# A two-layer encoder trunk on one core: the places of the tiles in SBUF

## The chip, the core and the metric

The kernel runs on one core of a Trainium2 chip. A core has five engines that run apart from each other and meet in semaphores: TensorE (PE in the profile; its loads of the stationary operand are listed apart, as PEld), VectorE (DVE), ScalarE (ACT), GpSimd (POOL) and SyncE (SP), which here issues all transfers. The operands lie in SBUF, 128 partitions with the same byte addresses in each; products land in eight PSUM banks. The metric is the time of one execution on the chip in microseconds, the median of several runs.

## The reference, cut to what matters

Two sequences of 256 tokens with 1024 features (512 tokens in all) go through two layers. All arithmetic is float32.

```python
for i in range(DEPTH):                       # 2
    h = rms_norm(x, norm_mix[i])
    kv = rms_norm(mem, norm_mem[i]) @ w_mem_kv[i]
    if i % 2 == 0:
        p = h @ a_w_in[j]                    # differential attention, 8 heads
        mixed = diff_mixer(p[..., :-X_WIDTH], ...); w_out = a_w_out[j]
    else:
        p = h @ b_w_in[j]                    # three dilated windows, 8 heads each
        mixed = dilated_mixer(p[..., :-X_WIDTH], ...); w_out = b_w_out[j]
    cross = memory_attention(xq, mk, mv)
    x = x + concatenate([mixed, cross]) @ w_out
    x = x + conv_ffn(rms_norm(x, norm_ffn[i]), w_up[i], conv_w[i], conv_b[i], w_down[i])
```

## The kernel before, in words

**Products.** A float32 number is kept as two parts, hi and lo, each in a format that TensorE takes in one pass. A product of two such numbers is three matmuls (`mm3`, L368 to L370): hi by hi, hi by lo, lo by hi. Nearly all matmuls are 128 rows by 128 columns of stationary operand with 512 columns of moving operand. In a row of the profile `acc<-wh,hl` the first name behind the arrow is the moving operand and the second the stationary one, which a weight load (PEld) brings into the array before.

**Tiles.** `hh` and `hl` (`const` pool, [128, 8, 512], 16 KB for each partition) hold hi and lo of the normalised, transposed activations. `X` is the residual. Everything else that TensorE reads in these products lies in numbered slots of the pool `pool`: 30 slots `blk` of 2 KB, six `wh` and six `wl` of 4 KB (hi and lo of a weight unit), three `raw` of 4 KB (the unit as it is loaded), and slots `qn`, `e`, `eT`, `on`, `sq`.

**The three kinds of product.** They differ in which tiles meet in the array:

- the projections (`proj`, `proj_first`): moving `wh`/`wl`, stationary `hh`/`hl` (rows `acc<-wh,hh`, `acc<-wl,hh`, `acc<-wh,hl`);
- the up products of the FFN (`up_products`): moving `hh`/`hl`, stationary `wh`/`wl` (rows `acc<-hh,wh`, `sc<-hl,wh` and so on);
- the down products of the FFN, the output projections and the products with the memory tokens: moving `wh`/`wl`, stationary `blk` (rows `acc<-wh,blk` and so on).

**Order.** Coroutines on estimated engine clocks (`Sched`) write out one fixed order for each engine when the program is built. Weight units (220 of 512 KB) are loaded ahead by SP, split by ACT (L345) and DVE (L347). Projections and attention are interleaved in both layers; the FFN stands by itself.

**Places.** A pool gives its tiles addresses one behind the other, rounded up to 32 bytes; `const` comes first, then `pool` (each slot at its first use), then `small`. Some 128 bytes of constants stand at 16384, so `const` begins at 16512.

Of the kernel before, what the change touches and what calls it, by code (L numbers as in the profile page):

```python
# [24 lines left out]
NFF = DFF // 128  # L25
# [12 lines left out]

# [1 line left out]
class Event:  # L40
# [53 lines left out]
class Slots:  # L94
    """Buffers of one kind, handed out in the order in which they come free."""

# [70 lines left out]

# [1 line left out]
def unit_plan():  # L169
    """[(name, layer, rows, cols)] of [128, 1024] units: row blocks x column ranges."""  # L170
    plan = []
# [26 lines left out]
    def granules(name, layer, halves):  # L198
        """halves of 256 columns, two at a time."""
        for i in range(0, len(halves), 2):  # L200
            cols = sum(halves[i:i + 2], [])
            if i + 1 < len(halves):
                for u in range(4):
                    plan.append((name, layer, range(2 * u, 2 * u + 2), cols))
            else:
                proj(name, layer, cols)
# [55 lines left out]
def trunk_kernel(ctx: ExitStack, tc: tile.TileContext, io: dict, out: bass.AP):  # L262
# [3 lines left out]
    const = ctx.enter_context(tc.tile_pool(name="const", bufs=1))  # L266
    pool = ctx.enter_context(tc.tile_pool(name="pool", bufs=1))
    small = ctx.enter_context(tc.tile_pool(name="small", bufs=6))
    psum = ctx.enter_context(tc.tile_pool(name="psum", bufs=1, space=bass.MemoryType.PSUM))
# [24 lines left out]

# [1 line left out]
    X = const.tile([128, NT, D], F32, name="X")  # L296
# [7 lines left out]

    ident = const.tile([128, 128], F32, name="ident")
    perm_fwd = const.tile([128, 128], F32, name="perm_fwd")
    perm_bwd = const.tile([128, 128], F32, name="perm_bwd")
    mask = const.tile([128, 2, 512], BF16, name="mask")
    mhalf = const.tile([128, 32], F32, name="mhalf")
    gcols = const.tile([128, 12], F32, name="gcols")  # L310
    subg = const.tile([128, 128], F32, name="subg")
    convT = const.tile([128, 2, 4, 2 * NFF], F32, name="convT")
    nc.vector.memset(mhalf, -0.5)
# [10 lines left out]

# [1 line left out]
    plan = unit_plan()  # L326
# [45 lines left out]

# [1 line left out]
    def row_scale(src, h):  # L374
        """1 / rms of the rows of src [two of [128, 512]]; h: two slots for the squares."""
        ss = sm(2, "ss")
        for j in range(2):
            nc.scalar.activation(h[j].v, src[j], AF.Square, scale=1.0 / 32, accum_out=ss[:, j:j + 1])  # L378
            t = S.op("ACT", c_act(512, 0, 1))
        yield t  # L380
        rstd = sm(1, "rstd")
        s1 = sm(1, "s1")
        nc.gpsimd.tensor_scalar(s1, ss[:, 0:1], ss[:, 1:2], EPS, ALU.add, ALU.add)  # L383
        nc.gpsimd.tensor_tensor(rstd, s1, mhalf[:, 0:1], ALU.pow)
        yield S.op("POOL", 0.6)
        return rstd

    def norm_transposed(src, gkey, ident_, evac, src_done=None):
        """src: two of [128, 512]; evac(j, bank) is a coroutine that empties a bank of 4 blocks."""
        g = gains[gkey]  # L390
# [45 lines left out]
    def norm_h(t, gkey, permuted, x_ev, h_ev):  # L436
        """normalises token tile t of X into columns of hh, hl."""
        yield x_ev
# [42 lines left out]

# [1 line left out]
    CH = 2  # L483

    def fan_out(t, bank, posts):
        """hands the halves of a bank to their parts; frees the bank behind the last."""
        left = [len(posts)]

        def done(te):
            left[0] -= 1  # L490
            if not left[0]:
                bank.done(te)

        for j, p in enumerate(posts):
            S.spawn(p(t, bank.v[:, 256 * j:256 * j + 256], done))

    def proj(name, posts, h_evs=None, permuted=False):
        """one or two halves of 256 columns; post(t, slice, done) is spawned for each token tile."""
        n = len(posts)
# [23 lines left out]
    def proj_first(name, posts, h_evs):  # L523
        """proj of two halves with units and token tiles in the order FIRST."""
        bks, ws, seen = {}, [], [0] * NT
# [20 lines left out]
    class QBlock:  # L546
        """two heads; a[h]: hi of head h on its own partitions, lo on the other head's."""

# [7 lines left out]
    class KBlock:  # L556
        """two heads; a[h]: hi of head h on all partitions; lo: both heads' lo on their partitions."""

# [10 lines left out]
    def block_evac(kind, bufs, tp, g):  # L569
        """empties a bank of two heads into its block."""  # L570
        if kind == "-":
# [24 lines left out]
    def qk_post(rope, gcol, kinds, ev):  # L596
        """rms norm per head, rope, transposes; ev gets the two feature-major blocks."""
        qns = [None] * 2
# [86 lines left out]

# [1 line left out]
    def mem_tiles(l, evs):  # L687
        """normalised, transposed memory tiles; evs[i] gets [(hi, lo)] of two banks."""
        t = yield from load_gain(("mem", l), io["norm_mem"][l])
# [55 lines left out]

# [1 line left out]
    def transpose_e(e, n):  # L747
        """e: slot whose first n blocks of 128 columns are transposed; returns the slot of the result."""
        eT = yield from eT_s.get()
# [12 lines left out]
    def seq_view(x, s, permuted):  # L762
        """columns of sequence s of a [128, 512] tile; (q, b, r) of the permuted order in natural places."""
        if permuted:
            return x.rearrange("p (s b q r) -> p s q b r", s=2, q=2, r=2)[:, s]
        return x[:, s * 256:s * 256 + 256]

    def evac_seq(src, hi, lo, s, permuted):
        """PSUM [128, 256] of sequence s to hi, lo."""
        if permuted:  # L770
# [7 lines left out]
    def out_T(o, cols, tiles, s, permuted):  # L778
        """blocks at cols[j][i] of the slot o (token tile i of sequence s) to feature-major tiles[j]."""
        tp = yield from tp_s.get()  # L780
# [25 lines left out]
    def softmax2(sc):  # L806
        """two softmax numerators of 256 keys; scores are negated."""
        v = sc.v.rearrange("p (m k) -> p m k", m=2)
# [15 lines left out]
    def scores(sc, parts):  # L824
        """parts: (column, q block, q columns, k block, k columns); the two heads side by side in the array."""
        for c, q, tq, k, ks in parts:
# [243 lines left out]

# [1 line left out]
    def add_x(ps, t, c, ev, last):  # L1072
# [34 lines left out]
    def out_proj_last(name, groups, x_evs):  # L1107
        """several row groups, sequence by sequence."""
        ws = []
# [27 lines left out]

# [1 line left out]
    def ffn_post(l, i, bks, ev):  # L1139
# [139 lines left out]

# [1 line left out]
    for t in range(NT):  # L1281
# [24 lines left out]
    S.spawn(start())  # L1306
    nlam = const.tile([128, 1], F32, name="nlam")
    ropes = {}

    def setup():  # L1310
# [9 lines left out]
        yield 18.0  # L1320
        # gains of q (scaled and negated) and k, feature-major; 1 on the rotated dims
        nc.vector.tensor_scalar(gcols[:, 0:6], gcols[:, 0:6], QS, None, ALU.mult)
# [6 lines left out]
        nc.vector.tensor_tensor(lampr, lampr, lv[:, :, 1, :], ALU.mult)  # L1329
        lams = sm(2, "lams")  # L1330
        nc.vector.tensor_reduce(lams, lampr, AX.X, ALU.add)
        yield S.op("DVE", 1.0)
        lame = sm(2, "lame")
        nc.scalar.activation(lame, lams, AF.Exp)
# [34 lines left out]
    for key in ("aq", "ak", "b0", "b1", "b2"):  # L1369
        ropet = const.tile([128, 2, 2, 2, 16], F32, name=f"rope_{key}")  # L1370
        ropes[key] = ropet
    def gc(*cols):
        return [gcols[:, c:c + 1] for c in cols]

    # columns of gcols: xq l0, xq l1, a_q, b_q0..2 | xk l0, xk l1, a_k, b_k0..2
    G_XQ, G_AQ, G_BQ = (0, 1), 2, (3, 4, 5)
    G_XK, G_AK, G_BK = (6, 7), 8, (9, 10, 11)

    def main():
        ev = S.event  # L1380
        # layer 0
        xq, mk, mv = ev(), ev(), ev()
# [29 lines left out]
        yield from ffn(0, h1, x2, mT, [qk_post(None, gc(G_XK[1], G_XK[1]), "kk", mk), v_post(mv)])  # L1412
        # layer 1
        cross = [ev(), ev()]
# [25 lines left out]
def constants():  # L1440
    """Arrays that depend on the shapes alone."""
    f = np.float32
    ident = np.eye(128, dtype=f)
    j = np.arange(128)
    # token j = a*16 + r16*4 + r4 of a tile goes to column r4*32 + r16*8 + a
    a, r16, r4 = j // 16, (j % 16) // 4, j % 4
    fwd = np.zeros((128, 128), f)
    fwd[j, r4 * 32 + r16 * 8 + a] = 1
    # permuted row j = r4*64 + r16*16 + a of a tile goes to column a*8 + r16*2 + r4
    r4, r16, a = j // 64, (j % 64) // 16, j % 16  # L1450
# [54 lines left out]
```

## Time and profile before

| | |
|---|---|
| median of 3 runs | 1450.37 us (1450.26 to 1450.9) |
| span of the profiled execution | 1447.8 us |
| median less that span | 2.6 us |
| PE busy | 1420.1 us, 98% |
| PEld, DVE, ACT, POOL busy | 81%, 58%, 44%, 23% |
| mean share of the DMA engines | 27.9% |

The profile gives one execution's span, from its first to its last instruction; what the measured time has beside it is the third row. A matmul is recorded from its start to its modelled end, 0.39 us for 512 columns, while the next one starts some 0.23 us later, so PE's busy share hides small gaps, and the pace is read from the starts.

### The profile page before, as it was taken

How to read it: one execution, taken by the hardware profiler on the slowest of the kernel's cores; microseconds unless marked ns; L12 is line 12 of the kernel's file. 1: busy time of each engine (PE TensorE's matmuls, PEld its weight loads, DVE VectorE, ACT ScalarE, POOL GpSimd, SP SyncE). 2: the span in 40 equal slices, each digit the busy share in tenths (PEclk: the TensorE clock that was granted, in tenths of full speed). 3: DMA queues.
4: the chain of work that ended last, by engine and by line, in shares of the span. 5: the costliest groups of instructions: out<-in, count | busy, mean ns of one | idle time of the engine just before them, and what ended most of it. 6: DMA issues, size and time to landing. Idle time of an engine off the chain costs nothing.

```text
span 1447.8 us, 19017 instructions
## 1 busy us (share of the span) xinstructions
PE 1420.1 (98%) x7168; PEld 1169.7 (81%) x7168; DVE 841.1 (58%) x1314; ACT 642.8 (44%) x1177; POOL 338.2 (23%) x652
## 2 busy tenths in 40 slices
PE   6999999999999999999999999999999999999999
PEld 4778888879888888878878878888888888888887
DVE  5777778886654355446666435444476563466353
ACT  5666555545442244244446434444554432243231
POOL 5836554121000000030154065445130000000000
PEclk9999999999999999999999999999999999999999
DMA  6531131123332332434221221112223233323221
GB/s 221 163 97 49 31 102 59 59 73 105 104 98 92 98 98 92 130 104 131 69 92 55 67 69 59 60 63 80 77 88 100 90 96 93 102 87 103 87 73 58
DMA packets 39260, 129.33 MB, mean 89 GB/s; under 512 B 4608, under 2 KB 5504, under 8 KB 39168
## 3 DMA queue, kind: packets, MB, share of 16 engines
q1 hardware_dynamic: 39168, 128.11, 27.9%
q8 instruction: 57, 0.93, 0.3%
q14 instruction: 35, 0.29, 0.1%
HBM read 126.00 MB, written 2.10 MB: 88 GB/s over the span
## 4 chain that ended last, share of the span: by engine, by line
PE 89%; POOL 4%; DVE 2%; issue 2%; DMA 1%; ACT 1%; SPq 0%; POOLq 0%; DVEq 0%; ACTq 0%
PE acc L368 18%; PE acc L370 17%; PE acc L369 17%; PE sc L370 7%; PE sc L368 7%; PE sc L369 7%; PE tp L752 2%; PE o L1035 2%; PE sc L832 1%; PE sc L830 1%; PE tp L651 1%; POOL rstd L617 1%; PE tp L412 1%; PE o L369 1%; PE o L368 1%
## 5 line engine op out<-in xcount | busy, mean ns | idle before, releaser
L347 DVE TENSOR_TENSOR wl<-raw,wh 128x1024 fp32r<-128x1024 f32 x220 | 273.0, 1244 | 247.5 <-ACT wh L345 246.8
L345 ACT CAST wh<-raw 128x1024 fp32r<-128x1024 f32 x220 | 230.8, 1050 | 367.2 <-PE sc L369 191.7
L368 PE MATMUL acc<-wh,hh 128*128 128x512 f32 (+1 forms) x536 | 218.3, 407 | 0.9 <-ACT hh L425 0.9
L369 PE MATMUL acc<-wl,hh 128*128 128x512 f32 (+1 forms) x536 | 204.8, 382 | 0.0
L370 PE MATMUL acc<-wh,hl 128*128 128x512 f32 (+1 forms) x536 | 204.7, 382 | 0.0
L368 PE MATMUL acc<-wh,blk 128*128 128x512 f32 x368 | 148.8, 404 | 0.0
L368 PE MATMUL acc<-hh,wh 128*128 128x512 f32 (+1 forms) x384 | 145.1, 378 | 0.0
L368 PE MATMUL sc<-hh,wh 128*128 128x512 f32 (+1 forms) x384 | 144.9, 377 | 0.0
L369 PE MATMUL sc<-hl,wh 128*128 128x512 f32 (+1 forms) x384 | 144.5, 376 | 0.0
L370 PE MATMUL acc<-hh,wl 128*128 128x512 f32 (+1 forms) x384 | 144.5, 376 | 0.0
L369 PE MATMUL acc<-hl,wh 128*128 128x512 f32 (+1 forms) x384 | 144.5, 376 | 0.0
L370 PE MATMUL sc<-hh,wl 128*128 128x512 f32 (+1 forms) x384 | 144.5, 376 | 0.0
L370 PE MATMUL acc<-wh,blk 128*128 128x512 f32 x368 | 143.8, 391 | 0.0
L369 PE MATMUL acc<-wl,blk 128*128 128x512 f32 x368 | 143.6, 390 | 0.0
L370 PEld LDWEIGHTS acc<-wh,hl 128*128 128x128 f32 x536 | 100.8, 188 | 21.8 <-DVE hl L427 0.3
L368 PEld LDWEIGHTS acc<-wh,hh 128*128 128x128 f32 x536 | 101.5, 189 | 18.8 <-ACT hh L425 1.3
L369 PEld LDWEIGHTS acc<-wl,hh 128*128 128x128 f32 x536 | 101.4, 189 | 15.5 <-DVE wl L347 0.5
L383 POOL TENSOR_SCALAR s<-ss 128x1 f32<-128x1 f32 x24 | 11.4, 476 | 434.1 <-ACT qn L378 428.5
L617 POOL TENSOR_TENSOR rstd<-ss,mhalf 128x4 f32<-128x4 f32 x96 | 106.2, 1106 | 8.0
L370 PEld LDWEIGHTS sc<-hh,wl 128*128 128x128 f32 x384 | 72.2, 188 | 14.6
L368 PEld LDWEIGHTS acc<-hh,wh 128*128 128x128 f32 x384 | 72.2, 188 | 14.6
L369 PEld LDWEIGHTS acc<-hl,wh 128*128 128x128 f32 x384 | 72.2, 188 | 14.5
(152 smaller groups left out, 2484.5 us busy)
## 6 DMA issues: line engine op xcount, KB each, us to landing
raw<-w SPq DMA_DIRECT2D x220, 512.0 KB, 3.6
blk<-mem SPq DMA_DIRECT2D x16, 256.0 KB, 6.5
y<-X SPq DMA_DIRECT2D x8, 256.0 KB, 2.0
X<-x SPq DMA_DIRECT2D x3, 512.0 KB, 8.9
blk<-norm_mix SPq DMA_DIRECT2D x4, 256.0 KB, 6.3
blk<-norm_mem SPq DMA_DIRECT2D x4, 256.0 KB, 6.2
blk<-norm_ffn SPq DMA_DIRECT2D x4, 256.0 KB, 5.1
X<-x SPq DMA_DIRECT2D x2, 256.0 KB, 3.0
```

The costliest lines, as they stand in the source:

```text
L345: nc.scalar.copy(hi.v, r.v)
L347: nc.vector.tensor_tensor(lo.v, r.v, hi.v.bitcast(F32), ALU.subtract)
L368: nc.tensor.matmul(out_, ah, bh, start=start, stop=False)
L369: nc.tensor.matmul(out_, ah, bl, start=False, stop=False)
L370: nc.tensor.matmul(out_, al, bh, start=False, stop=stop)
L412: nc.tensor.transpose(tp.v[:, k * 128:k * 128 + 128], h[j].v[:, k * 128:k * 128 + 128], ident_)
L617: nc.gpsimd.tensor_tensor(rstd, ss, mhalf[:, 0:4], ALU.pow)
L651: nc.tensor.transpose(tp.v[:, x * 128:x * 128 + 128], src[:, x % 2, b * 128:b * 128 + 128], ident)
L752: nc.tensor.transpose(tp.v[:, i * 128:i * 128 + 128], e.v[:, i * 128:i * 128 + 128], ident)
L830: nc.tensor.matmul(sc[h].v[:, c:c + n], q.a[h].v[:, tq], k.a[h].v[:, ks], start=True, stop=False)
L832: nc.tensor.matmul(sc[h].v[:, c:c + n], q.a[h].v[half(h), tq], k.lo.v[half(h), ks], start=False, stop=True)
L1035: nc.tensor.matmul(o[:, t, h, :], eT.v[:, i * 128:i * 128 + 128], vt[s].v[:, c:c + 64], start=(i == 0), stop=(i == 3))
```

## The change

The tiles get other places, and nothing else is altered but three small tiles. `const` now holds the identity and permutation tables, `gcols`, `nlam`, `mhalf` (4 columns in place of 32, and so a shorter MEMSET) and an unused `spacer`, then `X`, `hh`, `hl`. `mask`, `subg`, `convT` and the rope tables move into a new pool `tail` behind the slots. `lams` and `lame` get one buffer each in place of six.

```diff
     const = ctx.enter_context(tc.tile_pool(name="const", bufs=1))
     pool = ctx.enter_context(tc.tile_pool(name="pool", bufs=1))
+    tail = ctx.enter_context(tc.tile_pool(name="tail", bufs=1))
     small = ctx.enter_context(tc.tile_pool(name="small", bufs=6))
...
+    ident = const.tile([128, 128], F32, name="ident")
+    perm_fwd = const.tile([128, 128], F32, name="perm_fwd")
+    perm_bwd = const.tile([128, 128], F32, name="perm_bwd")
+    gcols = const.tile([128, 12], F32, name="gcols")
+    nlam = const.tile([128, 1], F32, name="nlam")
+    mhalf = const.tile([128, 4], F32, name="mhalf")
+    const.tile([128, 64], F32, name="spacer")
     X = const.tile([128, NT, D], F32, name="X")
...
-    ident = const.tile([128, 128], F32, name="ident")
-    perm_fwd = const.tile([128, 128], F32, name="perm_fwd")
-    perm_bwd = const.tile([128, 128], F32, name="perm_bwd")
-    mask = const.tile([128, 2, 512], BF16, name="mask")
-    mhalf = const.tile([128, 32], F32, name="mhalf")
-    gcols = const.tile([128, 12], F32, name="gcols")
-    subg = const.tile([128, 128], F32, name="subg")
-    convT = const.tile([128, 2, 4, 2 * NFF], F32, name="convT")
+    mask = tail.tile([128, 2, 512], BF16, name="mask")
+    subg = tail.tile([128, 128], F32, name="subg")
+    convT = tail.tile([128, 2, 4, 2 * NFF], F32, name="convT")
...
-    nlam = const.tile([128, 1], F32, name="nlam")
...
-        lams = sm(2, "lams")
+        lams = small.tile([128, 2], F32, bufs=1, name="lams")
...
-        lame = sm(2, "lame")
+        lame = small.tile([128, 2], F32, bufs=1, name="lame")
...
-        ropet = const.tile([128, 2, 2, 2, 16], F32, name=f"rope_{key}")
+        ropet = tail.tile([128, 2, 2, 2, 16], F32, name=f"rope_{key}")
```

The built programs place the tiles so (byte address in a partition, and what is left of it after whole multiples of 2048 and of 64):

| tile | before | mod 2048 | mod 64 | after | mod 2048 | mod 64 |
|---|---|---|---|---|---|---|
| `ident` | 32896 | 128 | 0 | 16512 | 128 | 0 |
| `X` | 16512 | 128 | 0 | 18432 | 0 | 0 |
| `hh` | 38592 | 1728 | 0 | 34816 | 0 | 0 |
| `hl` | 54976 | 1728 | 0 | 51200 | 0 | 0 |
| `blk0`, `wh0`, `wl0` | 73952, 90336, 94432 | 224 | 32 | 67584, 83968, 88064 | 0 | 0 |
| every other slot | | 224 | 32 | | 0 | 0 |

The slots follow each other in the same order as before. Each engine's order of instructions and waits is the same, but for the size of one MEMSET. VectorE's first rows of before (`qn`, `wl`, `hl` are the first normalised tile, the lo part of the first weight unit and the lo part of the activations):

```order
1 L313 MEMSET mhalf 128x32
2 L400 SCALAR_TENSOR_TENSOR qn_111<-X,rstd,blk_89 128x512
3 L347 TENSOR_TENSOR wl_104<-raw_94,wh_103 128x1024
4 L427 TENSOR_TENSOR hl<-tp_124,hh 128x4x128
5 L427 TENSOR_TENSOR hl<-tp_133,hh 128x4x128
6 L400 SCALAR_TENSOR_TENSOR qn_138<-X,rstd,blk_89 128x512
```

and the same place of the changed kernel:

```order
1 L316 MEMSET mhalf 128x4
2 L403 SCALAR_TENSOR_TENSOR qn_115<-X,rstd,blk_93 128x512
3 L350 TENSOR_TENSOR wl_108<-raw_98,wh_107 128x1024
4 L430 TENSOR_TENSOR hl<-tp_128,hh 128x4x128
5 L430 TENSOR_TENSOR hl<-tp_137,hh 128x4x128
6 L403 SCALAR_TENSOR_TENSOR qn_142<-X,rstd,blk_93 128x512
```

Line numbers grow by three and the running numbers of the tiles by four; no row has moved on any engine.

## Rows read from the trace of the kernel before

**Rows 1.** The page, busy time of each engine (us, share of the span, instructions).

```profile
PE 1420.1 (98%) x7168; PEld 1169.7 (81%) x7168; DVE 841.1 (58%) x1314; ACT 642.8 (44%) x1177; POOL 338.2 (23%) x652
```

**Rows 2.** The page, the chain that ended last, shares of the span by engine.

```profile
PE 89%; POOL 4%; DVE 2%; issue 2%; DMA 1%; ACT 1%; SPq 0%; POOLq 0%; DVEq 0%; ACTq 0%
```

**Rows 3.** The chain by line, in 0:60, 60:290, 340:590 and 720:1040 us.

```profile
by line: DMA raw<-w 24.4%; PE acc L370 10.9%; PE acc L368 10.9%; PE acc L369 10.9%; ACT wh L345 3.5%; PE sc L370 3.1%; PE sc L369 3.1%; PE sc L368 3.1%; PE tp L412 2.8%; issue 2.7%; DVE blk L584 2.5%; DVE hl L427 2.2%; ACT qn L378 2.1%; DVE
by line: PE acc L368 21.7%; PE acc L370 20.4%; PE acc L369 20.3%; PE sc L830 5.8%; PE o L938 5.5%; PE sc L832 5.5%; PE tp L752 4.8%; PE tp L651 3.2%; PE o L868 2.9%; issue 1.8%; PE tp L784 1.6%; PE tp L412 1.2%; ACT qn L378 0.6%; DVE e L927
by line: PE acc L370 16.7%; PE acc L369 16.7%; PE acc L368 16.7%; PE sc L369 14.8%; PE sc L370 14.8%; PE sc L368 14.8%; PE o L369 1.8%; PE o L370 1.8%; PE o L368 1.8%
by line: PE acc L368 19.4%; PE acc L370 18.4%; PE acc L369 18.4%; PE o L1035 7.1%; PE tp L752 5.4%; POOL rstd L617 4.9%; PE tp L651 3.0%; issue 2.8%; PE sc L832 2.4%; PE sc L837 2.2%; PE o L868 2.1%; PE sc L830 2.1%; POOL qn L636 1.4%; POOL
```

**Rows 4.** Groups by form: line, operation, out<-moving,stationary, shapes, count; busy us, mean ns.

```profile
L368 PE MATMUL acc<-wh,hh 128*128 128x512 f32 x472 | 199.7, 423 | 0.9 <-ACT hh L425 0.9
...
L368 PE MATMUL acc<-wh,blk 128*128 128x512 f32 x368 | 148.8, 404 | 0.0
...
L368 PE MATMUL sc<-hh,wh 128*128 128x512 f32 x320 | 126.7, 396 | 0.0
...
L368 PE MATMUL sc<-wh,blk 128*128 128x512 f32 x104 | 40.8, 393 | 0.0
...
L368 PE MATMUL o<-wh,blk 128*128 128x512 f32 x72 | 28.1, 390 | 0.0
...
L368 PE MATMUL acc<-hh,wh 128*128 128x256 f32 x64 | 18.5, 289 | 0.0
```

**Rows 5.** Windows: stretch, length, PE busy (matmuls), granted clock, DMA share, GB/s.

```profile
400.00:440.00 40.00, 40.00 (x173) 1.00 0.29 93
450.00:490.00 40.00, 40.00 (x178) 1.00 0.29 92
```

**Rows 6.** Timeline of PE, projections of layer 1: start us, us, engine, line, operation.

```profile
844.61 0.39 PE L369 MATMUL acc<-wl,hh 128*128 128x512 f32 x1
...
846.71 0.39 PE L369 MATMUL acc<-wl,hh 128*128 128x512 f32 x1
...
854.40 0.40 PE L369 MATMUL acc<-wl,hh 128*128 128x512 f32 x1
```

**Rows 7.** Timeline of PE, products with the memory tokens of layer 1.

```profile
646.88 0.39 PE L369 MATMUL acc<-wl,blk 128*128 128x512 f32 x1
...
648.96 0.39 PE L369 MATMUL acc<-wl,blk 128*128 128x512 f32 x1
...
651.46 0.39 PE L368 MATMUL acc<-wh,blk 128*128 128x512 f32 x1
```

**Rows 8.** Timeline of PE, a run of three projection matmuls between attention work.

```profile
107.57 0.48 PE L368 MATMUL acc<-wh,hh 128*128 128x512 f32 x1
...
108.35 0.60 PE L651 MATMUL tp<-ident,qn 128*128 128x128 f32 x4
```

**Rows 9.** Groups by form, one of a projection's three, in 720:1040 and in 60:290.

```profile
L369 PE MATMUL acc<-wl,hh 128*128 128x512 f32 x288 | 113.7, 395 | 0.0
...
L369 PE MATMUL acc<-wl,hh 128*128 128x512 f32 x141 | 55.7, 395 | 0.0
```

**Rows 10.** Groups by form, weight loads of `hh` and of `blk`.

```profile
L368 PEld LDWEIGHTS acc<-wh,hh 128*128 128x128 f32 x536 | 101.5, 189 | 18.8 <-ACT hh L425 1.3
...
L368 PEld LDWEIGHTS acc<-wh,blk 128*128 128x128 f32 x368 | 69.2, 188 | 12.6
```

**Rows 11.** Timeline of PE, projection with 256 moving columns.

```profile
1022.74 0.28 PE L368 MATMUL acc<-wh,hh 128*128 128x256 f32 x1
...
1024.72 0.28 PE L370 MATMUL acc<-wh,hl 128*128 128x256 f32 x1
```

**Rows 12.** The page's DMA issues (KB each, us to landing), and the start of VectorE's timeline.

```profile
raw<-w SPq DMA_DIRECT2D x220, 512.0 KB, 3.6
...
0.80 0.09 DVE L313 MEMSET mhalf<- 128x32 f32 x1 [0.80 <-PEq L1478]
```

## The prediction

> **What bounds the kernel now.** The page comes first: PE is busy 98% of the span, DVE 58%, ACT 44%, POOL 23% [rows 1]. A busy share of pipelined matmuls proves little, so the chain of waits is next: 89% of it is PE, the rest spread over POOL, DVE, ACT and DMA [rows 2]. By stretches the chain says where a shorter matmul would count [rows 3]. In the FFN (340 to 590 us) nothing but matmuls stands on it. In the first layer's projections (60 to 290) nearly all is PE. In the second layer's (720 to 1040) some 15% is POOL's `pow` and rope, `issue` and other engines. In the first 60 us about 40% is PE and 24% the landing of weights. So the pace of the matmuls sets the time nearly everywhere, and the question is whether a tile's place touches it.
>
> It seems to. [...] One holds 173 matmuls, the other 178 [rows 5]. A matmul is recorded for 0.39 us, so some 1.7 of each count began before the stretch: 40/171.3 = 233.5 ns for an up product, 40/176.3 = 226.9 ns for a down product. Both are 128 x 128 by 512 columns. What differs is the tiles: up products move `hh`/`hl` against `wh`/`wl`, down products move `wh`/`wl` against `blk`.
>
> A stricter pair has the same moving tiles, the same shape and the same kind of neighbours, and only the stationary tile differs. Projections (stationary `hh`) step 9 times in 2.10 us and then 33 times in 7.69: 233 ns, and never less [rows 6]. Products with the memory tokens (stationary `blk`), behind a break, step 9 times in 2.08 us, 231 each, and then 11 times in 2.50: 227 [rows 7]. They settle into a faster pace after about nine matmuls, and projections never do. The weight load of the next matmul runs beside each one and lasts 188 to 189 ns with either tile [rows 10], so it is not itself longer.
>
> By the table of places, `blk`, `wh` and `wl` all stand at 224 modulo 2048 (32 modulo 64) before, and `hh` and `hl` at 1728 (0 modulo 64). Where the moving and the stationary tile have the same remainder the pace settles at 227; where they differ by 32 modulo 64 it stays at 233, whichever of the two is the odd one. I read it as two streams of reads of the same memory, the moving operand and the next weights, which lock into a good rhythm only when they start in step. The trace cannot show the mechanism, only the pairing.
>
> [...]
>
> **The change part by part.** No instruction is added, removed or moved; one MEMSET gets narrower. After it `X`, `hh`, `hl` and all slots have remainder 0 modulo 2048, so all three kinds of product have the relation that only the third had. The price is 233.5 - 226.9 = 6.6 ns for each settled matmul, and 233 - 231 = 2 ns for each of the eight or nine before.
>
> *Up products*: two banks x three forms x 320 = 1920 [rows 4], in 8 long runs, so 1848 stand at the tenth place or later: 1848 x 6.6 ns + 64 x 2 ns = 12.3 us. All of it counts, since the chain of the FFN is PE alone.
>
> *Projections*: 3 x 472 = 1416 [rows 4], but the attention work cuts them up. Of 149 runs in the timeline 80 have three matmuls, as the one of [rows 8], and gain nothing to speak of. From 720 to 1040 there are 3 x 288 = 864 [rows 9], 465 at the tenth place or later and 321 in the eight before: 3.1 + 0.6 = 3.7 us, of which I keep 85%, PE's share of the chain: 3.2. From 60 to 290 there are about 422 [rows 9], with 120 and 242: 0.8 + 0.5 = 1.3, kept at 95%: 1.2. Before 60 us there are 93 and 50: 0.7, of which 0.3 for PE's 40%.
>
> *Half-width products* (256 columns): nine groups of 64, six of up products and three of projections [rows 4], 576 in all, step 17 times in 1.98 us, 116 ns each [rows 11]. Half the columns could give back half, 3.3 ns x 576 = 1.9 us; but the next weight load must fit into those 116 ns too, and that may set them: between 0 and 1.9, I take 0.6.
>
> *Down products* (3 x (368 + 104 + 72) = 1632 [rows 4]) and the attention's own matmuls keep their relation: 0. The transposes bring `ident` (128 modulo 2048, 0 modulo 64) against slots, out of step before and in step modulo 64 after; by the 3.3 ns of a half-width product some 700 of them could give 2 us, and I take 0.
>
> *Transfers*: the rows of `raw` begin at another place. They matter where their landing is on the chain, 24% of the first 60 us or 14.6 us [rows 3, 12]; later the loads run ahead. I take 0. [...]
>
> *VectorE, ScalarE, GpSimd*: the slots that they combine had one remainder among themselves before and have after, so at most X, `hh` and `hl` are new partners. None of these engines is the bound. The narrower MEMSET (0.09 us [rows 12]) stands 6 us ahead of DVE's next work: 0.
>
> The sum: 12.3 + 3.2 + 1.2 + 0.3 + 0.6 = 17.6 us. The profiled span is 1447.8 and the median 1450.37, so 2.6 us lie around the span; I leave them: 1450.4 - 17.6 = **1432.8 us**. If every matmul of the two slower kinds gained the 6.6 (1920 + 1416, or 22.0 us), with 1.9 and 2, it would be near 1424; if only the long FFN runs gain, 1438.
>
> **The rivals.**
>
> *The place does nothing* (chance 17%). The two paces would come from something else that goes with the kind of product. For it: each kind of product also has its own place in the program, and the trace has no case of `hh` in step. Against it: projections and memory products are alike in everything but the stationary tile. Then 1450 us, within 0.2% (about 3 us, what a measurement of this kernel can tell from no change). [...]
>
> *Slower: what helps is the odd 32, not the agreement* (11%). The only fast pair of before has both operands at 32 modulo 64, and the trace never shows both at 0. If an operand that begins at 0 modulo 64 costs the 6.6 ns by itself, the down products lose their pace: 1205 of their 1632 are settled, and 1205 x 6.6 = 8.0 us makes 1458; if the two operands' costs add, up products and projections lose another 6.6, some 17 us, and it is 1475. Against it: one odd operand costs the same whether it is the moving or the stationary one, which an agreement explains and two separate costs only by chance. It would show from the first down product, near 445 us.
>
> *Faster than the sum: a full step more* (10%). If starting on a round place takes off the same 6.6 ns a second time, all settled matmuls (1848 + 678 + 1205 = 3731) give up to 24.6 us more: about 1408. For it: the trace has single steps of 224 ns while the pace settles, so 227 is no floor. Against it: nothing shows such a pace held. [...]
>
> **How the numbers follow.** The sum holds with 62%; its own range is 1424 to 1438. No change has 17%, the slower rival 11%, the faster one 10%. Leaving out those last two leaves 79%, so the range runs from a little under the sum's lower bound, for a part of the second step, to the upper edge of no change: 1422 to 1453. Faster by over 0.2% (below 1447.5): 62 + 10 = 72%; within 0.2%: 17%; slower: 11%.
>
> **What would show it.** In the changed profile a gap-free 40 us of up products should hold 178 matmuls, as one of down products does, which stays at 178. A long run of projections should settle at 227 behind about nine matmuls; runs of three should not change. The FFN stretches should be shorter by 2.8%, the projections' by less than half of that, the first 60 us hardly. The prediction is wrong if up products still hold 173 in 40 us, or if down products fall below 178; and its size is wrong if POOL's `pow` takes more of the chain between 720 and 1040, which would mean that the projections' gain went into waits.

## The result and the profile after

The changed kernel takes 1434.4 us (median of 4 runs, 1433.39 to 1434.93) beside 1450.32 us for the kernel before (4 runs, 1449.88 to 1450.9). The ratio is 0.989, with a 95% interval of 0.9877 to 0.9903: 15.9 us faster, where 17.6 were forecast. The profiled spans are 1432.2 and 1447.8 us, 15.6 apart.

The page of the changed kernel, busy time of each engine and the chain that ended last, to be read beside [rows 1, 2]:

```profile
PE 1402.8 (98%) x7168; PEld 1171.2 (82%) x7168; DVE 841.1 (59%) x1314; ACT 644.5 (45%) x1177; POOL 338.4 (24%) x652
...
PE 87%; POOL 5%; DVE 3%; issue 2%; DMA 1%; ACT 1%; SPq 0%; POOLq 0%; DVEq 0%; ACTq 0%
```

Same counts, and the other engines are busy as long as before, to 2 us. PE alone lost 17.3 us of busy time. Its share of the chain fell by two points, which DVE and POOL took. The largest piece of that is in the first 60 us, where the three rows `PE acc` fell from 10.9% each [rows 3] to 4.6% and POOL's `rstd` came up:

```profile
by line: DMA raw<-w 24.9%; POOL rstd L620 13.5%; issue 5.0%; PE acc L373 4.6%; PE acc L371 4.6%; PE acc L372 4.6%; POOL ropew L638 4.4%; ACT wh L348 3.5%; POOL ss L619 3.5%; PE tp L415 2.8%; DVE blk L587 2.5%; POOL ropew L636 2.4%; DVE hl L
```

By this chain the shorter projections are no longer what the time waits for there.

The two stretches of [rows 5] in the changed kernel (PE alone: busy time, matmuls, granted clock, DMA share, GB/s):

```profile
400.00:440.00 40.00, 40.00 (x178) 1.00 0.34 94
450.00:490.00 40.00, 40.00 (x178) 1.00 0.33 99
```

The first holds up products, the second down products. Both now hold 178: up products went from 173 to 178 at the same clock, down products did not move. The DMA engines were busy for a larger share (0.34 and 0.33 for 0.29) than the bytes account for (94 for 93 GB/s and 99 for 92), which did no harm to the pace.

A long run of projections, which answers to [rows 6], and one of projections with 256 columns, which answers to [rows 11] (start us, us, engine, line, operation):

```profile
837.16 0.39 PE L372 MATMUL acc<-wl,hh 128*128 128x512 f32 x1
...
839.22 0.39 PE L372 MATMUL acc<-wl,hh 128*128 128x512 f32 x1
...
846.70 0.39 PE L372 MATMUL acc<-wl,hh 128*128 128x512 f32 x1
```

```profile
1013.36 0.28 PE L371 MATMUL acc<-wh,hh 128*128 128x256 f32 x1
...
1015.40 0.28 PE L373 MATMUL acc<-wh,hl 128*128 128x256 f32 x1
```

Nine steps in 2.06 us, 229 ns each, then 33 in 7.48: 226.7 ns, where [rows 6] showed 233 to the end. The half-width run did the opposite: 17 steps took 2.04 us, 120.0 ns each, against 1.98 and 116.5 before.

Where the 15.6 us came off is read from four matmuls: the first up product of either layer's FFN, and the first product of the last group of down products of either FFN. First the kernel before, then the changed one:

```profile
329.85 0.28 PE L368 MATMUL acc<-hh,wh 128*128 128x256 f32 x1
...
704.59 0.39 PE L368 MATMUL acc<-wh,blk 128*128 128x512 f32 x1
...
1075.17 0.28 PE L368 MATMUL acc<-hh,wh 128*128 128x256 f32 x1
...
1422.27 0.39 PE L368 MATMUL acc<-wh,blk 128*128 128x512 f32 x1
```

```profile
329.18 0.28 PE L371 MATMUL acc<-hh,wh 128*128 128x256 f32 x1
...
697.88 0.39 PE L371 MATMUL acc<-wh,blk 128*128 128x512 f32 x1
...
1065.83 0.28 PE L371 MATMUL acc<-hh,wh 128*128 128x256 f32 x1
...
1406.75 0.39 PE L371 MATMUL acc<-wh,blk 128*128 128x512 f32 x1
```

Layer 0's projections and attention gained 0.7 us, its FFN up to that last group 6.0 (374.74 to 368.70), layer 1's projections and attention 2.6 (370.58 to 367.95), its FFN 6.2 (347.10 to 340.92), the end 0.1.

Added up by kind over the whole trace, from each start to the next on PE, these are the same 15.6 us (but for rounding):

| matmuls | before, us | after, us | difference |
|---|---|---|---|
| up products, 512 columns (1920) | 448.1 | 435.5 | -12.6 |
| projections, 512 columns, and the waits behind them (1440) | 357.7 | 353.0 | -4.7 |
| down, output and memory products (1632) | 382.7 | 382.5 | -0.2 |
| up products and projections, 256 columns (576) | 70.5 | 71.5 | +1.0 |
| the attention's own matmuls and transposes, and the waits behind them | 176.5 | 177.6 | +1.1 |
| before PE's first matmul | 8.3 | 8.2 | -0.1 |

One trace is one execution, and terms with waits in them differ from one to the next: in the traces of this document's eight versions of the trunk PE's first matmul comes at 8.2 to 9.3 us, in no order of the layouts. The rows of up and half-width products repeat to 0.1 us in every kernel with the same remainders.

### The profile page after: what moved, and what is told of

Same layout as the page of the kernel before. It is cut to its first block, busy times and chain, and to the rows that moved or that the text cites. A ratio compares the mean times of both kernels' runs of the same rounds, so it can differ in the third digit from the quotient of the medians.

```text
span 1432.2 us, 19017 instructions
## 1 busy us (share of the span) xinstructions
PE 1402.8 (98%) x7168; PEld 1171.2 (82%) x7168; DVE 841.1 (59%) x1314; ACT 644.5 (45%) x1177; POOL 338.4 (24%) x652
## 4 chain that ended last, share of the span: by engine, by line
PE 87%; POOL 5%; DVE 3%; issue 2%; DMA 1%; ACT 1%; SPq 0%; POOLq 0%; DVEq 0%; ACTq 0%
PE acc L371 17%; PE acc L373 17%; PE acc L372 17%; PE sc L373 7%; PE sc L371 7%; PE sc L372 7%; PE tp L755 2%; POOL rstd L620 2%; PE o L1038 2%; PE sc L835 1%; PE sc L833 1%; PE tp L654 1%; PE tp L415 1%; PE o L371 1%; PE o L372 1%
## 5 line engine op out<-in xcount | busy, mean ns | idle before, releaser
L348 ACT CAST wh<-raw 128x1024 fp32r<-128x1024 f32 x220 | 231.9, 1055 | 357.6 <-PE sc L372 182.3
L373 PEld LDWEIGHTS acc<-hh,wl 128*128 128x128 f32 x384 | 72.3, 188 | 12.5
```

What stands on the lines that cost most here:

```text
L348: nc.scalar.copy(hi.v, r.v)
L373: nc.tensor.matmul(out_, al, bh, start=False, stop=stop)
```

## The experiments

**The pace by itself.** The forecast rested on the pairing of two remainders, of which the trace had only two cases. So `m1_sweep` leaves the trunk out and runs 60 matmuls of one form, twenty times, each behind four transposes (`brk`) that break the pace. `mov` and `sta` begin at 0 modulo 2048; `m` and `s` are the bytes by which the moving and the stationary operand start later.

```python
CASES = [("both_even", 0, 0), ("sta_half", 0, 32), ("mov_half", 32, 0), ("both_half", 32, 32),
         ("sta_word", 0, 4), ("sta_pair", 0, 8), ("sta_quad", 0, 16), ("sta_sixth", 0, 24),
         ("sta_three", 0, 48), ("sta_line", 0, 64), ("sta_nine", 0, 96), ("sta_double", 0, 128),
         ("sta_fourfold", 0, 256), ("sta_eightfold", 0, 512), ("mov_quad", 16, 0), ("mov_three", 48, 0),
         ("mov_line", 64, 0), ("both_quad", 16, 16), ("mov_double", 128, 0), ("both_word", 4, 4)]
...
nc.tensor.matmul(ps, sta[:, s // 4:s // 4 + 128], mov[:, m // 4:m // 4 + 512],
                 start=k == 0, stop=k == REP - 1)
```

> This kernel leaves the whole trunk out: 20 runs of 60 matmuls of 128 x 128 by 512 columns, four transposes ahead of each run, with the moving and the stationary tile each begun at a chosen byte behind a multiple of 2048. Agreement theory (the two starts must agree modulo 64): a settled pace near 227 ns where both begin at 0, both at 32 and both at 16, and where they differ by 64, 128, 256 or 512; near 233 where they differ by 32; differences of 4 to 24 bytes are open and should lie between 227 and 240. Absolute theory (the place of each operand counts by itself): both at 0 is 227, both at 32 is 233 or more. Nothing theory: one pace in all 20.

PE's timeline of `m1_sweep`, in which 60 equal matmuls stand in one row (start us, us from the first start to the last end):

```profile
40.87 14.23 PE L291 MATMUL mov_half<-mov,sta 128*128 128x512 f32 x60
55.30 13.88 PE L291 MATMUL both_half<-mov,sta 128*128 128x512 f32 x60
...
141.22 14.24 PE L291 MATMUL sta_line<-mov,sta 128*128 128x512 f32 x60
...
170.14 14.20 PE L291 MATMUL sta_double<-mov,sta 128*128 128x512 f32 x60
184.53 13.88 PE L291 MATMUL sta_fourfold<-mov,sta 128*128 128x512 f32 x60
...
241.47 14.00 PE L291 MATMUL mov_line<-mov,sta 128*128 128x512 f32 x60
...
284.27 14.51 PE L291 MATMUL both_word<-mov,sta 128*128 128x512 f32 x60
```

Most rows fall into two classes of 13.88 and some 14.2 us, 5.9 ns apart for each of 59 steps, settling included; `mov_line` lies between them and `both_word` above. Settled (start of the last less start of the 21st, by 39) the two classes are 226.7 and some 233 ns. Both operands on 32 bytes are as fast as both on 0: it is agreement, and the round place by itself gives nothing. The number in the prediction's "32 modulo 64" fell, though: 64 and 128 bytes apart are slow, 256 and 512 are fast.

`m2_sweep` is the same with other places and sizes. Its edit:

```diff
+CASES = [("agree", 0, 0, 512, 128), ("d_onesixty", 0, 160, 512, 128), ("d_oneninetytwo", 0, 192, 512, 128),
+         ("d_twotwentyfour", 0, 224, 512, 128), ("d_twoeightyeight", 0, 288, 512, 128), ("d_kilo", 0, 1024, 512, 128),
...
+            nc.tensor.matmul(ps[0:c, 0:n], sta[:, s // 4:s // 4 + c], mov[:, m // 4:m // 4 + n],
```

> No trunk: twenty runs of 60 matmuls of one form each, with other places, other numbers of stationary columns or of moving columns. If the two starts must agree modulo 256, the runs with the stationary operand 1024 bytes off settle at 226.7 ns, and those 160, 192, 224 or 288 bytes off and the moving one 224 off at 229 to 234; both at 64 hold 226.7, both at 8 and both at 48 some 230. [...] For 256 moving columns the trace of the changed kernel lets one expect that agreeing starts are no faster than starts 32 bytes apart, 116 to 124 ns for both; the prediction had up to 3.3 ns faster. 384 columns: 172 against 176 to 178.

PE's timeline of `m2_sweep`:

```profile
40.75 13.98 PE L294 MATMUL d_oneninetytwo<-mov,sta 128*128 128x512 f32 x60
54.92 14.24 PE L294 MATMUL d_twotwentyfour<-mov,sta 128*128 128x512 f32 x60
...
83.78 13.88 PE L294 MATMUL d_kilo<-mov,sta 128*128 128x512 f32 x60
...
154.99 14.06 PE L294 MATMUL narrow_agree<-mov,sta 128*64 128x512 f32 x60
169.24 14.14 PE L294 MATMUL narrow_half<-mov,sta 128*64 128x512 f32 x60
...
212.66 7.44 PE L294 MATMUL short_agree<-mov,sta 128*128 128x256 f32 x60
220.29 7.35 PE L294 MATMUL short_half<-mov,sta 128*128 128x256 f32 x60
227.83 7.26 PE L294 MATMUL short_mhalf<-mov,sta 128*128 128x256 f32 x60
235.28 10.65 PE L294 MATMUL mid_agree<-mov,sta 128*128 128x384 f32 x60
246.12 10.67 PE L294 MATMUL mid_half<-mov,sta 128*128 128x384 f32 x60
256.98 13.88 PE L294 MATMUL again_agree<-mov,sta 128*128 128x512 f32 x60
```

Both sweeps in one table, by the stationary start less the moving one, modulo 256 (512 columns, one operand on 0 unless the row says otherwise; settled ns):

| difference | settled, ns |
|---|---|
| 0 (0, 256, 512 and 1024 apart; both on 32; both on 64) | 226.7 |
| 192 (stationary 192 later, or moving 64 later) | 228.9 |
| 32, 48, 64, 96, 128, 160, 208, 224 | 232.2 to 234.4 |
| 4, 8, 16, 24, 240 | 230.6 to 233.3 |
| 0, but both on 4, 8, 16 or 48 | 237.8, 231.1, 230.1, 231.1 |

That 192 bytes of the one operand and 64 of the other give the same 228.9 fits a rule in which the difference modulo 256 counts, and not which operand is moved; so do the 233.4 of the stationary operand 32 or 288 later and the moving one 224 later. The last row says that agreement is not enough where the starts are no multiples of 32. No row of the table is faster than 226.7.

One expectation fell: 384 columns should have settled at 172 against 176 to 178; they settle at 173.3 with both relations. A stationary operand of 64 columns settles at 230.1 agreeing and 231.6 out of step, one of 32 columns at 231.7 and 240.0, where 128 agreeing had 226.7: fewer weight columns make the agreeing step no shorter, though their loads are recorded shorter (134 and 108 ns for 188). At 256 columns agreement costs, as was expected by then: 120.0 ns against 118.3 (stationary 32 later) and 116.8 (moving 32 later), which the prediction had the other way round.

**One part alone, and the change undone in part.** Three kernels ran together. `e1_hh_half` is the changed kernel with `hh` and `hl` alone put at 32 modulo 256, with the slots left at 0; `X` begins 256 bytes earlier:

```diff
-    const.tile([128, 64], F32, name="spacer")
...
+    const.tile([128, 8], F32, name="gap_a")
     hh = const.tile([128, KD, NTOK], F32R, name="hh")
     hl = const.tile([128, KD, NTOK], F32R, name="hl")
+    const.tile([128, 56], F32, name="gap_b")
```

> The changed kernel with hh and hl alone put 32 bytes out of step (32 modulo 64; all slots stay at 0 modulo 2048). Agreement theory: up products and long projection runs fall back to 233 ns, down products stay at 227, and the time goes back to 1450 (1448 to 1452). Absolute theory, in which round slots are what helps: part of the gain stays, since the slots are still round: 1438 to 1446. Nothing theory (another tile's place did it): 1434.

`e2_hh_only` is the kernel before with one line moved, by which `hh` and `hl` begin 32 bytes later, at 1760 modulo 2048 or 224 modulo 256, where the slots stand already. The slots, the masks and the tables stay:

```diff
+    nlam = const.tile([128, 1], F32, name="nlam")
     hh = const.tile([128, KD, NTOK], F32R, name="hh")
     hl = const.tile([128, KD, NTOK], F32R, name="hl")
...
-    nlam = const.tile([128, 1], F32, name="nlam")
```

> The kernel before with hh and hl alone moved, by 32 bytes, so that they agree with the slots at 32 modulo 64; no tile but these and nlam moves. Agreement theory: the whole gain of the change, 1434 (1432 to 1437), with up products at 227 ns. Absolute theory (both operands must begin at a round place): no gain, 1450, or a loss of up to 8 us. Nothing theory: 1450.

`e3_hh_line` is `e1_hh_half` with gaps of 16 and 48 floats, which puts `hh` and `hl` at 64 modulo 256:

```diff
-    const.tile([128, 8], F32, name="gap_a")
+    const.tile([128, 16], F32, name="gap_a")
...
-    const.tile([128, 56], F32, name="gap_b")
+    const.tile([128, 48], F32, name="gap_b")
```

> The changed kernel with hh and hl 64 bytes past a multiple of 128, slots at 0 modulo 2048. If the agreement has to hold modulo 64 only: 1434, as the change. If it has to hold modulo 128 or more: up products leave 227 ns and the time is between 1440 and 1450. If the multiples of 2 KB themselves help beyond the agreement, something between.

Measured, against 1450.65 us for the kernel before (15 runs):

| kernel | median, us | ratio, 95% |
|---|---|---|
| `e1_hh_half` | 1450.0 (11 runs) | 0.9993 (0.9984 to 1.0002) |
| `e2_hh_only` | 1435.71 (4 runs) | 0.9894 (0.988 to 0.9907) |
| `e3_hh_line` | 1442.35 (5 runs) | 0.9939 (0.9926 to 0.9953) |

Thirty-two bytes take the whole gain away, and thirty-two bytes in the kernel before give all of it. Masks and tables behind the slots, round places and the smaller `mhalf` are worth nothing that shows. In the third kernel the moving `hh` starts 64 later in up products, a difference of 192, and the stationary `hh` 64 later in projections, a difference of 64. By the sweep that is 228.9 and 233.3 ns, and the trace has just these. The up stretches of `e1_hh_half`, `e2_hh_only` and `e3_hh_line`:

```profile
400.00:440.00 40.00, 40.00 (x173) 1.00 0.31 93
```

```profile
400.00:440.00 40.00, 40.00 (x178) 1.00 0.33 97
```

```profile
400.00:440.00 40.00, 40.00 (x176) 1.00 0.32 93
```

**How far the agreement must go, and the other products.** `e4_mod256` keeps the slots and puts `hh` and `hl` 256 bytes down. `e5_blk_half` leaves `hh` and `hl` and puts the `blk` slots at 32 modulo 2048, in a pool of their own behind the other slots; those move by whole multiples of 2 KB, and the masks and tables behind them by 32 bytes. `e6_ident` moves `ident` and the permutation tables from 128 to 0 modulo 256, where the slots are:

```diff
-    const.tile([128, 64], F32, name="spacer")
...
     hl = const.tile([128, KD, NTOK], F32R, name="hl")
+    const.tile([128, 64], F32, name="gap_b")
```

```diff
+    bpool = ctx.enter_context(tc.tile_pool(name="bpool", bufs=1))
...
-    blk = slots("blk", N_BLK)
+    bpool.tile([128, 8], F32, name="gap")
+    blk = Slots(S, bpool, "blk", N_BLK, [128, 512])
```

```diff
+    const.tile([128, 32], F32, name="gap_i")
     ident = const.tile([128, 128], F32, name="ident")
...
-    const.tile([128, 64], F32, name="spacer")
+    const.tile([128, 32], F32, name="spacer")
```

> The changed kernel with hh and hl 256 bytes further down (1792 modulo 2048) and the slots where they are, so that they agree modulo 256 and no further. If agreement modulo 256 is what counts, the whole gain stays: 1434 us (1432 to 1437), ratio 0.989. If 512, 1024 or 2048 is needed, up products and projections fall back to 229 to 234 ns: 1440 to 1450.

> The changed kernel with the blk slots alone 32 bytes off, so that the products that bring them as the stationary operand (down, output and memory products) lose their agreement and the up products and projections keep theirs. Agreement: down products settle at 233 in place of 227, 1205 settled ones by 6.6 ns are 8.0 us, 1442 (1440 to 1444), with up products still at 227. If only the place of hh and hl matters, 1434 as the changed kernel.

> The changed kernel with ident and the two permutation tables 128 bytes further on, so that they too agree with the slots modulo 256; all else stays where it is. If agreement also quickens the 128-column transposes and permutations, 1432 or a little less (some 700 transposes by at most 3.3 ns are 2.3 us, part of it off the path); if it works on long runs of 512 columns alone, no change: 1434, ratio to before 0.989.

Measured, against 1450.7 us for the kernel before (9 runs):

| kernel | median, us | ratio, 95% |
|---|---|---|
| `e4_mod256` | 1435.15 (4 runs) | 0.9894 (0.9879 to 0.9909) |
| `e5_blk_half` | 1445.16 (5 runs) | 0.9963 (0.9951 to 0.9976) |
| `e6_ident` | 1433.75 (4 runs) | 0.9887 (0.9873 to 0.99) |

256 is enough; multiples of 2 KB are not needed. The two stretches of `e5_blk_half`, up and down:

```profile
400.00:440.00 40.00, 40.00 (x178) 1.00 0.31 93
450.00:490.00 40.00, 40.00 (x173) 1.00 0.31 92
```

The counts of [rows 5] stand here the other way round: down products are as slow as up products were. The time is 1 us above its range. The spans are 1442.1 and 1432.2, 9.8 apart before rounding, and from start to start the down, output and memory products alone took 392.4 us for 382.5. The eleventh and later ones of their runs hold 7.8 us of that, near the 8.0 expected. The second to tenth hold 1.1, and two runs ahead of layer 1's FFN end in waits that are longer by 0.9 and 0.7 us; neither was in the expectation. Other waits gave 0.5 us back. `e6_ident` shows no gain: the transposes of 128 columns stand 109 ns apart (median) with either place of `ident`.

The settled pace (ns, mean from the start of the eleventh and each later matmul of a run to the next start on PE, steps without a wait) gathers all the kernels:

| kernel | up | projections | down | up, 256 columns | projections, 256 |
|---|---|---|---|---|---|
| before | 233.3 | 233.3 | 226.7 | 118.3 | 116.7 |
| changed | 226.7 | 226.9 | 226.7 | 120.0 | 120.0 |
| `e1_hh_half` | 233.3 | 233.3 | 226.8 | 117.2 | 118.4 |
| `e2_hh_only` | 226.7 | 226.8 | 226.7 | 120.0 | 120.0 |
| `e3_hh_line` | 228.9 | 233.3 | 226.7 | 117.8 | 117.2 |
| `e4_mod256` | 226.7 | 226.8 | 226.7 | 120.0 | 120.0 |
| `e5_blk_half` | 226.7 | 226.9 | 233.3 | 120.0 | 119.9 |
| `e6_ident` | 226.7 | 226.9 | 226.7 | 120.0 | 120.0 |

**Which read meets which.** The prediction's picture was the moving operand of one matmul beside the weights of the next. `m3_turns` changes the starts by turns, so that either a matmul's own pair agrees or its moving operand with the next weights, and it runs bfloat16:

```diff
+CASES = [("agree", (0,), (0,), 512, F32R), ("turn_own", (0, 32), (0, 32), 512, F32R),
+         ("turn_next", (0, 32), (32, 0), 512, F32R), ("turn_mov", (0, 32), (0, 0), 512, F32R),
...
+            m, s = ms[k % len(ms)] // w, ss[k % len(ss)] // w
```

> No trunk again: runs of 60 matmuls in which the starts of the moving and the stationary operand change by turns between 0 and 32 bytes. If what must agree is the running matmul's moving operand and the weights that are loaded beside it for the next one, then turns in which each matmul's own two starts agree (own) settle at 233 ns and turns in which the moving start agrees with the next weights (next) at 226.7. If it is a matmul's own pair that counts, the other way round. Turns of one operand alone give about 230 by either. [...] For 256 columns starts that agree settle at 120.0 and starts 16, 64 or 128 bytes apart at 116 to 119.

PE's timeline of `m3_turns`:

```profile
26.15 14.17 PE L303 MATMUL turn_own<-mov,sta 128*128 128x512 f32 x60
40.51 14.07 PE L303 MATMUL turn_next<-mov,sta 128*128 128x512 f32 x60
54.76 14.05 PE L303 MATMUL turn_mov<-mov,sta 128*128 128x512 f32 x60
69.00 14.32 PE L303 MATMUL turn_sta<-mov,sta 128*128 128x512 f32 x60
83.52 13.89 PE L303 MATMUL agree_again<-mov,sta 128*128 128x512 f32 x60
97.68 13.11 PE L303 MATMUL bf_agree<-bmov,bsta 128*128 128x512 bf16 x60
111.07 13.11 PE L303 MATMUL bf_half<-bmov,bsta 128*128 128x512 bf16 x60
```

The settled paces are 231.7 (own), 230.0 (next), 230.0 (moving operand alone) and 234.9 (stationary operand alone, where some 230 was expected): neither pairing by turns reaches 226.7. The run does not tell the two apart, and the picture stays unproved. The second half is plain: bfloat16 settles at 215.8 to 215.9 ns in all six of its relations (0, 2, 16, 32 and 64 bytes apart for the stationary operand, 32 for the moving one). Its weight loads are recorded at 98 ns for 188. The shorter load alone does not explain the single pace, since the 4-byte loads of 108 ns (32 columns) in `m2_sweep` went with two; whether the element's size or something else of the type does, these runs do not say. Other 256-column relations (16, 64 and 128 apart) came out at 117.8 to 118.7 ns beside 120.0, as expected.

A version with the agreement for 512 columns and the other relation for 256 was not tried: at 2 to 3 ns for each of 576 matmuls (the table's 120.0 less 116.7 to 118.4) it could give 1 to 2 us by estimate, and the same slots would have to stand at two places.

## Why the prediction was right

- *The pairing.* That at 512 columns a pair of 4-byte operands with equal remainders settles at 227 and others at 233 held in every trace of the trunk but for `e3_hh_line`'s up products (228.9). What failed is the number beside it: "the same remainder" was read modulo 64, and it is 256. In the kernel before `hh` stood at 192 and the slots at 224 modulo 256, and the change puts all at 0 modulo 2048, which covers both numbers, so the forecast came to the same. A layout with `hh` 64 bytes from the slots would have been forecast as whole, and `e3_hh_line` gained half; by the sweep, where 128 bytes apart is in the row of 232.2 to 234.4 ns, one 128 bytes away would gain next to nothing.
- *Up products*: 12.3 forecast, 12.6 measured, all of it on the chain, as `e3_hh_line` and the FFN's edges show. The sentence that the FFN stretches would be shorter by 2.8% did not fit the sum: that is the up products' pace alone; with their unchanged down products the two FFN stretches lost 1.6 and 1.8%.
- *Projections*: 4.7 forecast after the shares of the chain, 4.7 measured with the waits (24 more of them, whose rows write `sc`, were left out of the 1416). Inside it two errors met. The gain starts at the fourth matmul behind a break: the fourth to tenth gave 1.4 us, 4.1 ns each where I had set 2, and the settled ones 4.1 us. Of these 5.5 us some 0.8 went into waits between them, a smaller share than I had taken off. That the sums agree to 0.1 us is luck: the same projections and waits took 351.9 to 354.7 us in the traces of the five kernels that have them in step, 3.0 to 5.8 less than before, and most of that spread is waits before 60 us. The stretch up to the first FFN gained 0.7 where 1.5 stood: its projections gave 1.2, the half-width ones took 0.3 back, the attention's own work and the transposes before 60 us 0.5, and PE began 0.1 earlier.
- *Half-width products*: 0.6 gained forecast, 1.0 lost. This is the term with the wrong sign, and 1.6 of the 2.0 us between the sum of 17.6 and the spans' 15.6; another 1.1 is the waits below, which had no term, and the up products, the down products and PE's start gave some 0.6 more than their terms. My lower bound was "nothing"; no row excluded a loss, and I had let the two relations order 256 columns as they order 512. Nor did a weight load have to fit into the 116 ns: at 256 columns each is recorded at 0.19 us and the next begins 0.12 us after it, with either relation, so they overlap. What sets the step there no run shows.
- *Down products, transposes, transfers at 0*: -0.2 us, no change of the transposes' 109 ns, and nothing clear of noise that `e2_hh_only`, which leaves the slots and so `raw` where they were, lacks beside the changed kernel. The 4 KB packets of the first 60 us took 183.4 and 185.7 ns on average with `raw` at 224 modulo 256 (before and `e2_hh_only`) and 176.7 to 183.6 in the six kernels with it at 0, two ranges that overlap; the landing of weights has 24 to 26% of the chain there in all eight.
- *Waits*: the attention's own matmuls and transposes took 1.1 us longer, 0.7 of it in layer 1. There the five kernels with projections in step lost 0.6 to 0.9 us and the two others with projections out of step nothing (0.1 at most), so it goes with the agreement. The chain of the first 60 us goes over POOL's `rstd` (13.5%) in the same five and not in the other two. Before the transposes of `qn` PE sat idle 4.3 us and now 5.6, of which POOL's `qn` has 3.7 (3.3 before) and DVE's 1.4 (0.5 before); first before, then changed:

```profile
L651 PE MATMUL tp<-ident,qn 128*128 128x128 f32 x192 | 29.4, 274 | 4.3 <-POOL qn L636 3.3 <-DVE blk L584 0.5 <-DVE qn L621 0.5
...
L654 PE MATMUL tp<-ident,qn 128*128 128x128 f32 x192 | 29.4, 274 | 5.6 <-POOL qn L639 3.7 <-DVE qn L624 1.4 <-DVE blk L587 0.5
```

- *The signs.* 178 up products and 178 down products in 40 us came as named, and so did 227 ns in the long projection runs. In the runs of three the steps stayed at 231.9 ns (231.8 before). POOL's `rstd`, the `pow` of the text, has 5.0% of the chain between 720 and 1040 us for 4.9%, so hardly any of the projections' gain there went into it.
- *The rivals.* That the place does nothing is refuted by `e1_hh_half` and `e2_hh_only` together. That an odd 32 is what helps is refuted by the changed kernel's down products, 178 in 40 us on round places, and by `both_half`. The full step more did not come: agreeing starts keep 226.7 on 0, 32, 64 and 224.

## What to carry to other kernels

Where long runs of matmuls with 4-byte operands and 512 moving columns set the time, let the moving and the stationary tiles begin at the same remainder modulo 256, on multiples of 32 (226.7 ns a step in the sweeps, 228.9 to 237.8 otherwise): here one declaration moved by a line gave all of a 1% gain. Read it from the starts, not from busy shares: two gap-free stretches of the same shape with 173 and 178 matmuls are the whole clue. And a relation found at one size is measured at the other sizes before it is given a sign there.

## What the runs showed that I had not expected

- In agreement the settled step grows by some 53.3 ns for each 128 columns more: 120.0 ns for 256, 173.3 for 384, 226.7 for 512. Bfloat16 is 10.9 ns below that at 512 columns (215.8). Out of step it is 6.6 ns more at 512 (233.3), the same at 384 (173.3), and 1.3 to 3.3 less at 256 (116.7 to 118.7), so agreement fixes a step rather than the shortest one.
- Fewer stationary columns make a 4-byte matmul no faster: 230.1 ns with 64 and 231.7 with 32, beside 226.7 with 128, all in agreement.
- 4-byte starts that are both 4 bytes past a round place settle at 237.8 ns, slower than any pair out of step with as many columns on either side (234.4 at most).
- What in the chip makes 256 the period, and which two reads meet, stays open.
